# Layer B of a two-layer encoder trunk: the value projection as seven half-size products, and keys split once and doubled by transfers inside SBUF

## The chip, the cores and the metric

The kernel runs on one core of one Trainium2 chip. The metric is device time in microseconds (us) of one execution; lower is better. The engines are named as the profile names them: PE (TensorE, matrix products), DVE (VectorE), ACT (ScalarE), POOL (GpSimd) and SP (SyncE, which issues transfers). Each has an instruction queue of its own and works through it strictly in order.

## The reference, cut to what matters

The input is 512 tokens of width 1024, in float32. Layer A (sparse attention and a squared-ReLU MLP) comes first. Layer B then works on the residual stream `h`:

```
k, v, f_logit = split(rms_norm(h, g_kv) @ w_kv)      # 512x1024 @ 1024x2064
cum = cumsum(log_sigmoid(f_logit + b_f))             # one value per head and token
q = rms_norm(h, g_attn_b) @ w_q                      # 16 heads of 64
logits = q @ k.T / 8 + cum[t] - cum[s], causal       # per head
h = h + (softmax(logits) @ v) @ w_o
h = h + square(relu(rms_norm(h, g_mlp) @ w_up)) @ w_down
```

and a last RMS norm gives the output. The value projection is `v = x @ w_v` with x of 512x1024 and w_v of 1024x1024.

## The kernel before, in words

**Three passes for one product.** Matrix operands are float32r. To keep float32 accuracy each operand is split into a high part (rounded to float32r) and a low part (the rest), and `mm3` issues three matmuls: high by high, high by low, low by high. A split costs one pass of ACT (the high part) and one of DVE (the low part). For weights there is a second way, switched by `lows(stage)`: ACT writes the high part and its negative, and a POOL transfer that adds on arrival (`wlo<-raw`) makes the low part in SBUF.

**What sets the order.** `body` only records operations. `Recorder.schedule` (a list scheduler with cost estimates per operation, priorities from PE's order, and pools of SBUF slots and PSUM banks) then writes the final order of every engine's queue, and `emit` issues them. All instructions therefore carry one source line, L416, in the profile, and are told apart by the names of their tiles.

**Layer B, in the order of PE's work.**

- `afterA` (line 1055) ends layer A's MLP: it normalises h, transposes it through PSUM (`yT`), and splits it twice, into `xq` (scaled with g_attn_b) and `xk` (scaled with g_kv). Both show as `xT` in the profile.
- The query projection (`qp`, `qo`), then the 16 forget-gate logits (`fb`).
- The value projection (line 1108 on): `tokprod` twice, for columns 0 to 511 and 512 to 1023. Each half takes 8 chunks of k, 4 tiles of 128 tokens, 3 passes: 96 matmuls of 128x512. Results (`tp`) are split into `vb`; head pair 4 also gets an unsplit copy `vbf`.
- On DVE, in the meantime, the forget-gate chain: `z`, `e`, `s`, `w2` and their polynomial, then the running sum `cum`. `cum` goes to DRAM (`cd`), comes back as a row per head broadcast over partitions (`ck`), and is transposed on PE (`cb`, `cq`).
- `bias(head)`: POOL makes the decay and mask `bt` from `ck` and `cq`, four `TENSOR_SCALAR` and four `AFFINE_SELECT` a head.
- `kproj(p)`, for 8 pairs of heads: 24 matmuls into `kp`. The logits of a head contract over 128 partitions that hold the 64 rows of k twice (once for the high, once for the low part of q). So each head's 64 rows of `kp` are written to both halves of a tile `kdup`, split into high and low: per pair four ACT casts and four DVE subtractions of 64x512.
- `attn(p)`: logits (`lg`, 8 matmuls a head, 128 to 512 columns wide), sum and minimum on DVE (`l<-lg,bt`), exponent on ACT, reciprocal (`rc`) on DVE, scaling on POOL (`l<-l,rc`), transposes on PE (`pT`), a split (`ph`, `pl`) by ACT and DVE, and the product with v (`pv`, 8 matmuls a head).
- The output projection: 192 matmuls `tp<-whi,qo` and `tp<-wlo,qo`, which also fill PE's gaps in the later pairs. Then layer B's MLP, whose down projection already runs as seven products.

Of the kernel before, what the change touches and what calls it, by code (L numbers as in the profile page):

```python
# [15 lines left out]
T = 512  # L16
# [109 lines left out]
class Recorder:  # L126
# [294 lines left out]
CFG = {  # L421
# [8 lines left out]
def body(ctx, tc, a, out):  # L430
# [19 lines left out]
    p_ps = pool("ps", 8, bass.MemoryType.PSUM, reach=CFG["ps"])  # L450
    p_dr = {n: pool(n, 1, bass.MemoryType.DRAM) for n in ("hd", "cd")}
# [45 lines left out]
    def lows(stage):  # L497
        lo_eng[0] = G if stage in CFG["dl"] else V
# [180 lines left out]
    def unpair(dst, b, scale):  # L679

        up, dn = slice(0, 64), slice(64, 128)
        S.activation(dst[up, 0], b[up], AF.Copy, scale=scale)
# [128 lines left out]
    oT = new_xT("oT")  # L811
    topk(1)
    qprod(1, 0)
    for t in range(NT):
# [3 lines left out]
        for kv in range(4):  # L818
# [38 lines left out]
            else:  # L857

                pv, u, o = bank([128, 4, 128], "pv"), scr([64, 4, 128], "u"), scr([128, 2, 128], "o")
# [6 lines left out]
            split(oT[0][kv][:, :, c], oT[1][kv][:, :, c], o)  # L866
# [16 lines left out]
    mT = None  # L883

    def proj_o(oT, w, g, first):
        tokprod(xl(oT), w, 0, 8, 0, 512, addto(0), order=first)
# [5 lines left out]
        tokprod(xl(oT), w, 0, 8, 512, 512, last, order="t")  # L892
        return xT

    lows("oa")
    xT = proj_o(oT, a["w_o_a"][0], g, "t")


    def mlp(xT, wu, wd, after, last=False):
        lows("up1" if last else "up0")  # L900
        H = T // 2
        tl = [slice(0, H), slice(H, T)]

        share = [htile([128, 512], "share") for _ in range(2)]

        def add(o, b, x):
            V.tensor_tensor(o, b, x, op=OP.add)

        def xop(src):
            out = []  # L910
            for k in range(0, 4, 2):
                hl = tuple(rec.tile(p_x8, [128, 2, H], F32R, n) for n in ("xhi", "xlo"))
                split(hl[0], hl[1], src[:, k:k + 2, :])
                out.append(hl)
            return out

        def wop(src):
            out = []
            for y in src:
                hl = rec.tile(p_wh, [128, 2, 512], F32R, "dhi"), rec.tile(p_wl, [128, 2, 512], F32R, "dlo")  # L920
                split(hl[0], hl[1], y)
                out.append(hl)
            return out

        def sub(o, p, q):
            for x, y, z in zip(o, p, q):
                V.tensor_tensor(x, y, z, op=OP.subtract)

        def part(b, x, w, start, i, c=slice(0, 512), js=range(2)):

            for j in js:
                for k in (2 * j, 2 * j + 1):
                    mm3(b[:, c], tuple(u[:, k % 2, 128 * i:128 * i + 128] for u in x[j]),
                        tuple(u[:, k % 2, c] for u in w[j]), start and k == 0, k == 3, skip_group_check=True)

        def prod(bs, x, w, start, whole=False):
            if whole:
                for i in range(2):
                    part(bs[i], x, w, start, i)
            else:  # L940
                for j in range(2):
                    for i in range(2):
                        part(bs[i], x, w, start, i, js=(j,))

        def banks():
            return [bank([128, 512], "tp") for _ in range(2)]

        for ci in range(4):
# [26 lines left out]
            def raw(j, n):  # L975
                ys = []
                for k in range(f0 + 512 * j, f0 + 512 * j + 512, 256):
                    ys.append(rec.tile(p_wr, [128, 2, 512], F32, "raw"))
# [353 lines left out]
```

## Time and profile before

| | |
|---|---|
| time, median of 3 runs | 1167.9 us (1167.73 to 1167.95) |
| the profiled execution's own time | 1168.06 us |
| its span, first to last instruction | 1166.2 us |
| PE, DVE, ACT, POOL busy, share of the span | 98%, 66%, 64%, 20% |
| value projection on PE | 623.6 to 668 us |
| layer B's attention on PE, first logits to last `pv` | 678.5 to 790.5 us |
| last matmul of the output projection | 825.7 us |

A row of the profile's timeline gives start, duration, engine, line, operation, output<-inputs, the tile's shape and how many stand together; in brackets, how long the engine had been idle and who released it. Matmuls overlap each other: their listed duration (about 390 ns for 128x512) is longer than the distance from one start to the next, so PE's busy share reads near 100% even where it does less than it could. The distance between starts is the number to price a matmul with.

### The profile page before, as it was taken

Reading aid. Unit: us, or ns where it says so; the run is one execution under the profiler, and the core shown is the slowest. Engines: PE = TensorE matmul, PEld = TensorE weight load, DVE = VectorE, ACT = ScalarE, POOL = GpSimd, SP = SyncE. Lnnn points to the kernel's source line nnn. Section 1 sums busy time; section 2 is a strip of 40 time slices with the busy share of each in tenths; the row PEclk is TensorE's granted clock in tenths of the full one; section 3 lists DMA queues with packets and bytes.
Section 4 is the critical chain, followed back from the end, with each engine's and each line's share of the span. In section 5 each row is a group of like instructions: output and inputs, shape, how many; then the busy total and the mean of one; then the engine's idle time right before and its main releaser. Section 6 shows DMA issues by size and latency. Waiting matters only on the chain. (4 is left out here: it accounts for less than half of the span.)

```text
span 1166.2 us, 16382 instructions
## 1 busy us (share of the span) xinstructions
PE 1141.8 (98%) x5687; PEld 948.6 (81%) x5687; DVE 771.8 (66%) x1489; ACT 741.6 (64%) x1396; POOL 236.5 (20%) x391
## 2 busy tenths in 40 slices
PE   8999999999999999999999999999999999999997
PEld 7777787898888888888887878788988888888885
DVE  7899998455736656468656359773568357465596
ACT  8852899665745556559573259996568356465562
POOL 0311454110200200201010068961101002002001
PEclk9999999999999999999999999999999999999999
DMA  9841363782982964957875313768719819739501
GB/s 341 184 91 55 110 181 70 148 235 59 241 242 64 256 186 123 269 150 176 234 173 124 110 37 115 207 169 179 204 68 240 248 56 248 219 88 255 198 19 73
DMA packets 145315, 187.86 MB, mean 161 GB/s; under 512 B 8104, under 2 KB 92096, under 8 KB 145232
## 3 DMA queue, kind: packets, MB, share of 16 engines
q1 hardware_dynamic: 129680, 130.18, 35.5%
q0 software_dynamic: 15552, 56.63, 25.2%
q8 instruction: 45, 0.74, 0.3%
q14 instruction: 38, 0.31, 0.1%
HBM read 125.94 MB, written 4.23 MB: 112 GB/s over the span
## 5 line engine op out<-in xcount | busy, mean ns | idle before, releaser
L416 PE MATMUL up<-xT,whi 128*128 128x512 f32 (+1 forms) x1152 | 323.7, 366 | 0.0
L416 PEld LDWEIGHTS up<-xT,whi 128*128 128x128 f32 x1152 | 207.9, 189 | 34.9
L416 POOL DMA_DIRECT2D wlo<-raw x108 | 95.1, 881 | 692.6 <-ACT wlo L416 339.2
L416 DVE TENSOR_TENSOR dlo<-raw,dhi 128x1024 fp32r<-128x1024 f32 x112 | 136.5, 1227 | 144.5 <-ACT dhi L416 90.3
L416 PE MATMUL up<-xT,wlo 128*128 128x512 f32 (+1 forms) x576 | 210.0, 366 | 0.0
L416 PE MATMUL tp<-dhi,xhi 128*128 128x512 f32 (+1 forms) x452 | 171.9, 390 | 1.2 <-DVE h L416 0.8
L416 PE MATMUL tp<-dlo,xhi 128*128 128x512 f32 (+1 forms) x452 | 171.4, 387 | 0.0
L416 PE MATMUL tp<-dhi,xlo 128*128 128x512 f32 (+1 forms) x452 | 170.8, 388 | 0.0
L416 ACT CAST whi<-raw 128x1024 fp32r<-128x1024 f32 (+2 forms) x124 | 123.9, 1026 | 72.9 <-DMA raw<-in_w_up_dram 63.1
L416 ACT CAST dhi<-raw 128x1024 fp32r<-128x1024 f32 x112 | 116.4, 1047 | 67.1 <-PE up L416 64.1
L416 PE MATMUL tp<-whi,xT 128*128 128x512 f32 (+2 forms) x432 | 125.2, 371 | 2.7 <-DVE r L416 1.6
L416 ACT ACTIVATE wlo<-whi 128x1024 fp32r<-128x1024 f32 x108 | 112.4, 1059 | 20.8 <-DMA wlo<-raw 10.3
L416 PEld LDWEIGHTS up<-xT,wlo 128*128 128x128 f32 x576 | 108.3, 189 | 17.5
L416 DVE TENSOR_TENSOR h<-tp,h 128x512 f32<-128x512 f32 (+1 forms) x97 | 64.7, 680 | 79.0 <-PE tp L416 78.9
L416 PEld LDWEIGHTS tp<-dhi,xhi 128*128 128x128 f32 x452 | 84.8, 188 | 21.7 <-DVE h L416 1.4
L416 PEld LDWEIGHTS tp<-dhi,xlo 128*128 128x128 f32 x452 | 84.7, 188 | 17.3
L416 PEld LDWEIGHTS tp<-dlo,xhi 128*128 128x128 f32 x452 | 84.9, 188 | 16.8
L416 PEld LDWEIGHTS tp<-whi,xT 128*128 128x128 f32 x432 | 77.0, 188 | 14.7 <-ACT whi L416 3.4
L416 DVE TENSOR_TENSOR raw<-raw 128x1024 f32<-128x1024 f32 x64 | 76.6, 1220 | 18.3 <-DMA raw<-in_w_down_dram 17.6
L416 ACT ACTIVATE r<-up 128x512 f32<-128x512 f32 x64 | 37.9, 592 | 79.6 <-PE up L416 79.6
L416 POOL TENSOR_SCALAR l<-l,rc 128x128 f32<-128x128 f32 (+3 forms) x128 | 69.9, 574 | 52.7 <-DVE rc L416 38.3
L416 PE MATMUL tp<-wlo,xT 128*128 128x512 f32 (+2 forms) x216 | 78.4, 372 | 0.5 <-DVE ra L416 0.5
(191 smaller groups left out, 1928.7 us busy)
## 6 DMA issues: line engine op xcount, KB each, us to landing
wlo<-raw POOLq DMA_DIRECT2D x108, 512.0 KB, 8.8
raw<-in_w_down_dram SPq DMA_DIRECT2D x96, 512.0 KB, 10.9
raw<-in_w_up_dram SPq DMA_DIRECT2D x64, 512.0 KB, 7.1
raw<-in_w_kv_b_dram SPq DMA_DIRECT2D x16, 512.0 KB, 6.8
raw<-in_w_in_a_dram SPq DMA_DIRECT2D x12, 512.0 KB, 8.6
raw<-in_w_o_a_dram SPq DMA_DIRECT2D x8, 512.0 KB, 4.4
raw<-in_w_q_b_dram SPq DMA_DIRECT2D x8, 512.0 KB, 7.6
ck<-cd SPq DMA_DIRECT2D x16, 256.0 KB, 3.7
```

What stands on the lines that cost most here:

```text
L416: getattr(self.engs[o.eng], o.fn)(*a, **k)
```

## The change

Two things are changed in layer B; layer A's code is only regrouped into shared helpers (`xop`, `wop`, `part`, `prod` leave `mlp`), and the two output projections keep their old form (`p7` holds only "v").

First, keys. `kproj` splits the 128 rows of a pair once into `kn`, high and low (one ACT cast and one DVE subtraction of 128x512), and four transfers from SBUF to SBUF on SP's queue write each head's 64 rows to both halves of `kdup`.

Second, the value projection. x is cut into blocks X[i,j] (token half i, k half j) and w_v into Y[j,n]; `proj7` forms seven products of 256x512 by 512x512 (24 matmuls each) from sums and differences of blocks, and adds the results. It needs the normalised input unsplit as well: `afterA` writes it to `xv` by 16 more ACT passes from PSUM. Products 1, 2 and 4 use blocks of the existing split `xk`. Weight blocks are combined in place (`raw<-raw`) and split into `dhi`, `dlo`; for products 3, 7 and 4 the low part comes by POOL's transfer. Blocks overwritten by a combination are loaded again (14 loads of 512 KB, before 8).

```diff
 CFG = {
+    "pw": 700, "p7": ("v",), "swap": False, "dup": True,
+    "far": ("v3", "v7", "v4"),
...
+    def wop(src, far=False):
+        out = []
+        for y in src:
+            hl = rec.tile(p_wh, [128, 2, 512], F32R, "dhi"), rec.tile(p_wl, [128, 2, 512], F32R, "dlo")
+            if far:
+                S.copy(hl[0], y)
+                S.activation(hl[1], f32(hl[0]), AF.Copy, scale=-1.0)
+                G.dma_start(hl[1], y, accum_op=OP.add)
+            else:
+                split(hl[0], hl[1], y)
+            out.append(hl)
+        return out
...
+    def proj7(X, ops, w, c0, stage, first, parts, done):
+        far = lambda n: (stage + n) in CFG["far"]
+
+        def op(i, j):
+            return ops[i, j] if ops else xop(X[i, j])
+
+        def raw(j, n):
+            return wraw(w, 0, j, c0 + 512 * n)
+
+        y11 = raw(0, 0)
+        b = banks(p_pw)
+        prod(b, op(0, 0), wop(y11, far("1")), True)
+        for i in range(2):
+            first(i, b[i])
+        prod(b, op(0, 1), wop(raw(1, 0), far("2")), False, True)
+        for i in range(2):
+            done(i, 0, b[i])
+        s1, s2 = ([rec.tile(p_s4, [128, 2, H], F32, n) for _ in range(2)] for n in ("s1", "s2"))
+        each(OP.add, s1, X[1, 0], X[1, 1])
+        sub(s2, s1, X[0, 0])
+        sub(X[1, 0], X[0, 0], X[1, 0])
+        sub(X[0, 1], X[0, 1], s2)
+        sub(y11, raw(0, 1), y11)
+        y22 = raw(1, 1)
+        sub(y22, y22, y11)
+        e = banks(p_pw)
+        prod(e, xop(s2), wop(y22, far("6")), True)
+        for i in range(2):
+            parts(2 + i, 0, e[i])
+        prod(e, xop(s1), wop(y11, far("5")), False)
+        for i in range(2):
+            parts(2 + i, 1, e[i])
+        z22 = raw(1, 1)
+        prod(e, xop(X[0, 1]), wop(z22, far("3")), False, True)
+        for i in range(2):
+            done(i, 1, e[i])
+        y12 = raw(0, 1)
+        sub(y12, z22, y12)
+        b = banks(p_pw)
+        prod(b, xop(X[1, 0]), wop(y12, far("7")), True)
+        for i in range(2):
+            done(2 + i, 1, b[i])
+
+        y21 = raw(1, 0)
+        sub(y21, y21, y22)
+        prod(b, op(1, 1), wop(y21, far("4")), False, True)
+        for i in range(2):
+            done(2 + i, 0, b[i])
...
+    xv = [big([128, 2, T], "xv", F32) for _ in range(4)] if "v" in CFG["p7"] else None
...
+                for i in range(2 if xv else 0):
+                    S.activation(xv[k // 2][:, i, c], b[:, i, :], AF.Copy, scale=gkv[:, k + i:k + i + 1])
...
+    def vfirst(i, b):
+        m1[i] = htile([128, 512], "m1")
+        S.copy(m1[i], b)
+
+    def vpart(t, n, b):
+        pt[t, n] = htile([128, 512], "vp")
+        add(pt[t, n], b, m1[t - 2])
...
+        if CFG["dup"]:
+
+            kn = htile([128, 2, T], "kn", F32R)
+            split(kn[:, 0, :], kn[:, 1, :], b)
+            for e in range(2):
+                for o in range(2):
+                    SP.dma_start(f32(ks[e])[64 * o:64 * o + 64], f32(kn)[64 * e:64 * e + 64])
+            return ks
```

The scheduler rewrites the order of all engines between 560 us and 826 us of the old profile; on PE the instructions of the first 2650 or so and of the last 1711 stand as before. Three places matter below.

PE, where the value projection has ended and the attention begins (`kp` is the key projection, `cb` the transposes of `cum`, `lg` the logits). Before, with 192 value matmuls and 7 of `kp` ahead of it:

```order
L416 MATMUL kp<-xT,whi 128x512
L416 MATMUL cb<-ident,cum 128x16
L416 MATMUL kp<-xT,whi 128x512
L416 MATMUL cb<-ident,cum 128x16 x2
L416 MATMUL kp<-xT,wlo 128x512
L416 MATMUL cb<-ident,cum 128x16
L416 MATMUL kp<-xT,whi 128x512 x2
```

In the changed kernel, with 168 value matmuls and 49 of `kp` ahead:

```order
L416 MATMUL kp<-xT,whi 128x512
L416 MATMUL cb<-ident,cum 128x16 x4
L416 MATMUL lg<-kdup,qo 128x128 x2
L416 MATMUL lg<-kdup,qo 128x256 x2
L416 MATMUL lg<-kdup,qo 128x384 x2
L416 MATMUL kp<-xT,whi 128x512
L416 MATMUL kp<-xT,wlo 128x512
```

`cb` has moved from the 200th to the 218th place after the forget-gate logits, and the first logits follow it at once instead of 36 matmuls later. At the first `pT` 70 matmuls of `kp` were done before, 112 now.

DVE, at the end of the forget-gate chain. Before, the chain stood nearly alone, with two value splits in its last steps:

```order
L416 TENSOR_TENSOR e<-e,s 16x512
L416 TENSOR_TENSOR vb<-tp,vb 128x8x64
L416 TENSOR_TENSOR z<-z,e 16x512
L416 TENSOR_TENSOR vb<-tp,vb 128x8x64
L416 SCALAR_TENSOR_TENSOR cum<-z,zrow 16x512
L416 TENSOR_TENSOR vb<-tp,vb 128x8x64 x2
```

In the changed kernel it stands behind and between the additions of the seven products (`vp`), all value splits and the first key split:

```order
L416 TENSOR_TENSOR vp<-tp,vp 128x512
L416 TENSOR_TENSOR e<-e,w_6665 16x512
L416 TENSOR_TENSOR vb<-vp,vb 128x8x64
L416 TENSOR_SCALAR e<-e 16x512
L416 TENSOR_TENSOR vb<-vp,vb 128x8x64
...
L416 TENSOR_TENSOR kn<-kp,kn 128x512
...
L416 SCALAR_TENSOR_TENSOR cum<-z,zrow 16x512
L416 TENSOR_TENSOR wlo<-raw,whi 128x1024
L416 TENSOR_TENSOR kn<-kp,kn 128x512
```

Between the first `vp` and `cum` stand 4 `wlo`, 10 additions, 6 `vb` and one `kn` beside the chain itself.

SP, the transfers around `cum`. Before:

```order
L416 DMA raw<-in_w_kv_b_dram 128x8x128 x3
L416 DMA cd<-cum 16x512
L416 DMA ck<-cd 128x512 x2
L416 DMA raw<-in_w_kv_b_dram 128x8x128
L416 DMA ck<-cd 128x512 x2
```

In the changed kernel:

```order
L416 DMA raw<-in_w_kv_b_dram 128x8x128 x5
L416 DMA kdup<-kn 64x1024 x4
L416 DMA raw<-in_w_kv_b_dram 128x8x128
L416 DMA cd<-cum 16x512
L416 DMA kdup<-kn 64x1024 x4
L416 DMA ck<-cd 128x512 x5
```

The first `ck` now stands behind the four transfers of the second pair's keys, which wait for `kn`, which DVE writes two instructions after `cum`.

## Rows read from the trace of the kernel before

**Rows 1.** The page's first part: each engine's busy time, share of the span and instructions.

```profile
PE 1141.8 (98%) x5687; PEld 948.6 (81%) x5687; DVE 771.8 (66%) x1489; ACT 741.6 (64%) x1396; POOL 236.5 (20%) x391
```

**Rows 2.** Busy time by stretch: bounds and length in us, then busy us and instructions of PE, PE's weight loads, DVE, ACT, POOL, the granted clock (1.00 is full), the DMA engines' share and GB/s. The stretches are the second half of the query projection, the value projection, the start of the attention, the attention, and the rest of the output projection.

```profile
585.00:624.00 39.00, 38.90 (x221) 32.84 (x220) 18.58 (x36) 29.99 (x48) 6.38 (x8) 1.00 0.76 166
624.00:668.00 44.00, 44.00 (x195) 36.42 (x195) 26.34 (x37) 9.30 (x16) 0.00 (x0) 1.00 0.43 112
668.00:690.00 22.00, 19.96 (x95) 16.05 (x94) 12.42 (x27) 9.93 (x21) 14.37 (x35) 1.00 0.19 49
690.00:790.00 100.00, 97.90 (x557) 80.65 (x557) 81.17 (x217) 94.87 (x229) 76.81 (x165) 1.00 0.52 148
790.00:826.00 36.00, 35.94 (x170) 29.60 (x169) 14.72 (x37) 23.45 (x46) 6.60 (x8) 1.00 0.72 152
```

**Rows 3.** The chain of work that ended last: start, us, what.

```profile
716.45 1.27 PE pv L416 x8
...
750.98 4.72 PE pv L416 x16
...
790.78 21.34 PE tp L416 x94
```

**Rows 4.** PE's timeline: the first value matmul, the first logits, the first transpose of the attention, a block of eight transposes and the instruction after it, the last `pv` pair, and the first matmul of layer B's MLP.

```profile
623.59 0.40 PE L416 MATMUL tp<-whi,xT 128*128 128x512 f32 x1
...
678.50 0.33 PE L416 MATMUL lg<-kdup,qo 128*128 128x128 f32 x2
...
689.20 0.65 PE L416 MATMUL pT<-ident,l 128*128 128x128 f32 x4 [2.04 <-POOL l L416]
...
773.45 1.08 PE L416 MATMUL pT<-ident,l 128*128 128x128 f32 x8
774.28 0.68 PE L416 MATMUL lg<-kdup,qo 128*128 128x256 f32 x3
...
790.33 0.33 PE L416 MATMUL pv<-ph,vb 128*128 128x256 f32 x1
...
825.88 0.40 PE L416 MATMUL up<-xT,whi 128*128 128x256 f32 x2
```

**Rows 5.** Groups of instructions from 664 to 792 us: engine, operation, tiles, shapes and count, then busy us and mean ns of one, then idle us before them and who ended it.

```profile
L416 POOL TENSOR_SCALAR l<-l,rc 128x512 f32<-128x512 f32 (+3 forms) x64 | 36.1, 593 | 18.4 <-DVE rc L416 17.3 <-PE pT L416 1.0
L416 POOL TENSOR_SCALAR bt<-ck,cq 128x512 f32<-128x512 f32 (+3 forms) x64 | 34.6, 568 | 53.8 <-ACT cq L416 48.8 <-DVE mn L416 3.1 <-DVE pl L416 1.0
...
L416 DVE TENSOR_TENSOR kdup<-kp,kdup 64x512 fp32r<-64x512 f32 x32 | 22.0, 688 | 12.6 <-ACT kdup L416 12.1
...
L416 POOL TENSOR_SCALAR_AFFINE_SELECT bt<-bt 128x128 f32<-128x128 f32 x64 | 18.9, 340 | 0.1
L416 ACT CAST kdup<-kp 64x512 fp32r<-64x512 f32 x32 | 18.6, 581 | 11.6 <-PE kp L416 9.2 <-DVE kdup L416 2.1
```

**Rows 6.** DVE's timeline: the start of the forget-gate chain, a weight split and what follows it, the running sum, two value splits.

```profile
624.40 0.74 DVE L416 SCALAR_TENSOR_TENSOR z<-fb,bfc,f 16x512 f32<-16x512 f32 x1 [1.05 <-ACT f L416]
...
635.63 1.21 DVE L416 TENSOR_TENSOR wlo<-raw,whi 128x1024 fp32r<-128x1024 f32 x1
636.77 0.41 DVE L416 TENSOR_SCALAR e<-e 16x512 f32<-16x512 f32 x1
...
645.29 1.20 DVE L416 TENSOR_TENSOR_SCAN cum<-z,zrow 16x512 f32<-16x512 f32 x1
646.42 1.25 DVE L416 TENSOR_TENSOR vb<-tp,vb 128x512 fp32r<-128x512 f32 x2
```

**Rows 7.** Instructions by tile over the whole run (count: least/median/most ns, first and last start): the MLP's split of combined weights on DVE and ACT, its split of combined inputs, and ACT's scaling of the transposed input out of PSUM.

```profile
L416 DVE TENSOR_TENSOR dlo<-raw,dhi x112: 1210/1225/1721, 247.8 to 1136.2; 128x1024 fp32r<-128x1024 f32 x112
...
L416 ACT CAST dhi<-raw x112: 1032/1047/1058, 246.7 to 1121.2; 128x1024 fp32r<-128x1024 f32 x112
...
L416 DVE TENSOR_TENSOR xlo<-s,xhi x32: 678/683/687, 291.7 to 1132.5; 128x512 fp32r<-128x512 f32 x32
...
L416 ACT ACTIVATE xT<-yT,gkv x16: 475/514/541, 567.8 to 591.1; 128x256 fp32r<-128x256 f32 x16
```

**Rows 8.** Transfers: the page's issues (count, KB each, median us from issue to landing), then for `ck` alone the issue's own ns and the least, median and longest landing.

```profile
wlo<-raw POOLq DMA_DIRECT2D x108, 512.0 KB, 8.8
raw<-in_w_down_dram SPq DMA_DIRECT2D x96, 512.0 KB, 10.9
...
raw<-in_w_kv_b_dram SPq DMA_DIRECT2D x16, 512.0 KB, 6.8
...
L416 SPq DMA_DIRECT2D ck<-cd x16: 319/361/1917, 648.1 to 749.4; - x16
...
DMA to landing us min/median/max: 3.2/3.7/8.0
```

**Rows 9.** POOL's timeline: its first work of the attention, and its last scaling.

```profile
670.70 4.15 POOL L416 TENSOR_SCALAR bt<-ck,cq 128x512 f32<-128x512 f32 x8 [48.75 <-ACT cq L416]
674.81 2.01 POOL L416 TENSOR_SCALAR_AFFINE_SELECT bt<-bt 128x128 f32<-128x128 f32 x8
676.81 2.63 POOL L416 TENSOR_SCALAR bt<-ck,cq 128x512 f32<-128x512 f32 x5
...
782.48 2.06 POOL L416 TENSOR_SCALAR l<-l,rc 128x512 f32<-128x512 f32 x4 [1.97 <-DVE rc L416]
```

**Rows 10.** SP's waits from 600 to 800 us: waiting queue, who was waited for, us in total, times, longest.

```profile
SPq L416 <- DVE cum L416: 25.5, 1, 25.5
```

More of the change, by code (lines that the diff above doesn't have):

```diff
@@ L808, in topk @@
         V.tensor_scalar(m, m, -3.2e38, NEG, op0=OP.is_gt, op1=OP.mult)
-    oT = new_xT("oT")
+    oT = [big([128, 2, T], "oT", F32) for _ in range(4)] if "oa" in CFG["p7"] else new_xT("oT")
     topk(1)
@@ new lines, in wop, with each @@
+    def wop(src, far=False):
+        out = []
+        for y in src:
[6 more added lines that the diff above has]
+                split(hl[0], hl[1], y)
+            out.append(hl)
+        return out
+    def each(op, o, p, q):
+        for x, y, z in zip(o, p, q):
+            V.tensor_tensor(x, y, z, op=op)
@@ new lines, in sub, with part, prod @@
+    def sub(o, p, q):
+        each(OP.subtract, o, p, q)
+    def part(b, x, w, start, i, c=slice(0, 512), js=range(2)):
+        for j in js:
+            for k in (2 * j, 2 * j + 1):
+                mm3(b[:, c], tuple(u[:, k % 2, 128 * i:128 * i + 128] for u in x[j]),
+                    tuple(u[:, k % 2, c] for u in w[j]), start and k == 0, k == 3, skip_group_check=True)
+    def prod(bs, x, w, start, whole=False):
+        if whole:
+            for i in range(2):
+                part(bs[i], x, w, start, i)
+        else:
+            for j in range(2):
+                for i in range(2):
+                    part(bs[i], x, w, start, i, js=(j,))
@@ new lines, in proj_o, with addh, first, done @@
+    def proj_o(X, w, g, stage):
+        xT = new_xT()
+        m1 = [htile([128, 512], "m1") for _ in range(2)]
+        def addh(t, n, b):
+            o = h[t][:, 512 * n:512 * n + 512]
+            add(o, b, o)
+        def first(i, b):
+            S.copy(m1[i], b)
+            for t, n in ((i, 1), (2 + i, 0), (2 + i, 1)):
+                addh(t, n, m1[i])
+        def done(t, n, b):
+            addh(t, n, b)
+            if (t, n) in ((0, 1), (1, 1), (2, 0), (3, 0)):
+                norm_T(h[t], rstd(h[t]), g, xT, t)
+        proj7(X, None, w, 0, stage, first, addh, done)
+        return xT
@@ L887, in proj_o, with proj_d @@
+    quad = lambda x: {(i, j): [x[2 * j + k][:, :, tl[i]] for k in range(2)] for i in range(2) for j in range(2)}
+    def proj_d(lhs, w, g, order):
+        tokprod(lhs, w, 0, 8, 0, 512, addto(0), order=order)
         xT = new_xT()
@@ L891, in last @@
             norm_T(h[t], rstd(h[t]), g, xT, t)
-        tokprod(xl(oT), w, 0, 8, 512, 512, last, order="t")
+        tokprod(lhs, w, 0, 8, 512, 512, last, order="t")
         return xT
-    lows("oa")
-    xT = proj_o(oT, a["w_o_a"][0], g, "t")
+    if "oa" in CFG["p7"]:
+        xT = proj_o(quad(oT), a["w_o_a"][0], g, "oa")
+    else:
+        lows("oa")
+        xT = proj_d(xl(oT), a["w_o_a"][0], g, "t")
     def mlp(xT, wu, wd, after, last=False):
         lows("up1" if last else "up0")
-        H = T // 2
-        tl = [slice(0, H), slice(H, T)]
         share = [htile([128, 512], "share") for _ in range(2)]
[L906 to L946, printed above, removed]
         for ci in range(4):
@@ L1244, in attn @@
                 V.tensor_tensor(o[64 * e:64 * e + 64], pv[0:64], u, op=OP.add)
-        split(qo[p][:, 0, :], qo[p][:, 1, :], o)
+        if not oB:
+            split(qo[p][:, 0, :], qo[p][:, 1, :], o)
+        elif p in CFG["pvb"]:
+            S.copy(oB[p // 2][:, p % 2, :], o)
+    oB = [big([128, 2, T], "oB", F32) for _ in range(4)] if "ob" in CFG["p7"] else None
     kss = {0: kproj(0)}
```

112 lines of the change are left out of this document (77 added, 35 removed).

## The prediction, made before the changed kernel ran

> **What bounds the kernel now.** I read first the page's part on engines and then the windows by stretch. PE is busy for 98% of the span [rows 1], and the granted clock is 1.00 (the 2.4 GHz level) in all five stretches [rows 2], so the change has no clock term. Then PE's own timeline, for where that busy time holds work and where it holds waiting. All that changes on PE lies between the first value matmul at 623.59 us and the first `up` at 825.88 us: 202.3 us [rows 4].
>
> Prices: a 512-column matmul costs 21.34/94 = 0.227 us, a head's 8 `pv` 1.27 (0.159 each; a head's 8 `lg` have the same columns), pair 4's 16 `pv` 4.72 [rows 3], a `pT` (774.28 - 773.45)/8 = 0.104 [rows 4]. I price `cb` and `yT` like `pT`. Work: (192 value + 192 `kp` + 192 output projection) x 0.227 = 130.75; 16 heads of `lg` 20.3; 14 of `pv` 17.8; 4.7; 160 `pT` 16.6; 16 `yT` 1.7; 4 `cb` 0.4. Sum 192.25. So 10 us of the 202.3 are lost, and where they are lost decides how much of a saving arrives. Up to the first `pT` at 689.20, 262 matmuls (192 value, 70 `kp`) 59.5, 18 `lg` 2.85 and `cb` 0.4 give 62.75 of 65.6: 2.85 lost, 2.04 of it the wait for POOL's first `l` [rows 4]. After it, 129.5 of 136.7: 7.2 lost. Behind the last `pv` at 790.33 stand 146 matmuls and the `yT`, 34.85 of 35.55, so 6.5 of the 7.2 belong to the attention. There ACT is busy for 94.9, DVE for 81.2 and POOL for 76.8 of 100 us [rows 2].
>
> **The change part by part.** *Value products.* 24 matmuls less: 24 x 0.227 = 5.45 us off PE.
>
> *What feeds them.* Between 585 and 668 us DVE is busy for 18.58 + 26.34 = 44.9 of 83 us, ACT for 39.3 [rows 2]. DVE gains 8 weight combinations and 8 `dlo`. The trace has no two-input DVE instruction on raw weights alone; `dlo`, 1.23 us in the median [rows 7] and 1.14 by distance between starts (636.77 - 635.63, a `wlo` of the same size, [rows 6]), bounds it from above, and half of that is the least I can argue from the `vb` splits of half the size, 1.25/2 = 0.63 [rows 6]. I take 1.14 since the size is the same: 16 x 1.14 = 18.2. Input combinations and their low parts are 16 of 128x512: x 0.63 = 10.1 (by the row's own 0.683 [rows 7], 10.9). Ten additions read from PSUM: x 0.63 = 6.3. Together 34.6, so 79.5 of the 77.6 us that remain: DVE is full, and what doesn't fit lands on the forget-gate chain, next term. ACT gains 16 `xv` x 0.51, 8 `xhi` x 0.6 (a cast of this size is between the 0.51 and the 0.581 of [rows 7, 5]), four weight passes x 1.05 [rows 7] and two `m1`: 18.4 on 39.3, which fits. One hazard on PE: product 2 waits for ACT's copy `m1`, which in ACT's queue stands behind a `dhi` whose block is re-loaded late; a re-load lands 6.8 us after issue [rows 8]. I take 0.5 us for it, bounds 0 and 2.
>
> *The forget-gate chain.* `cum` on DVE ends at 646.4 today, 22.1 us after `z` [rows 6], with PE far from needing it. Chain without two `wlo` (2.3) and the two `vb` (1.25): 18.5. In the changed order there stand behind the first `vp` 4 `wlo` 4.6, 10 additions 6.3, 6 `vb` 3.8 and a `kn` 0.7. The first `vp` needs the 72nd value matmul: 623.6 + 72 x 0.227 = 639.9; 639.9 + 33.9 = 673.8 if the whole chain were behind it, and a microsecond more for waits between small instructions. PE comes to `cb`, the 218th, at 623.6 + 217 x 0.227 = 672.9. So the added wait is 2 us (0 if part of the chain slips ahead of the first `vp`; 4 if `vp` banks come late). Behind `cb` PE has all logits queued, so nothing fills it.
>
> *`ck` and POOL's start.* SP's wait for `cum` is 25.5 us long [rows 10] and moves with it: `cd` issues at about 675. The first `ck` then stands behind four `kdup` transfers, which wait for `kn`, 1.14 (`wlo`) + 0.7 later, and cost four issues of 0.36 [rows 8]: `ck` at 678.3, landed at 682.0 (3.7), at worst 686.3 (8.0). POOL needs 4.15 + 2.01 + four of the next five `bt` at 0.53 (2.63/5), 2.1 [rows 9], and a scaling 0.6: the first `l` is done near 691, at worst 695. PE is at its first `pT` after (168 + 112) x 0.227 + 22 `lg` 3.5 + 0.4 = 67.5 of work, at 691.1, plus 2 + 0.5 of waits and the 0.8 that is lost there today without a named wait: 694.4. So POOL doesn't bind at the median, and the 2.04 wait goes in exchange for the one at `cb`.
>
> The transfers' order weighs against this change by a rule too. SP's queue sat 25.5 us at one transfer for `cum` [rows 10]. The Trainium skill ("DMA: Bandwidth & Descriptors", section "Anatomy of one DMA — SWDGE (gpsimd) path") says that the DMA engines do not wait on semaphores and any wait happens on the issuing sequencer before dispatch; the trace agrees. By that rule the `ck` row pays for `kn` though it doesn't need it; without the rule it would land some 3.3 us sooner, still ahead of PE's need.
>
> *Keys.* A pair's four DVE subtractions of 0.688 become one, and four ACT casts of 0.581 one [rows 5]; by size I take the same for 128 rows. Six pairs fall after 690: DVE -12.4, ACT -10.3 us. The 32 transfers of 256 KB go between SBUF tiles, which the trace doesn't show: nearest rows are `ck` (3.7) below and `w_down` (10.9) above [rows 8]; a gain is excluded, since today no transfer stands there. I take 4, as the size is `ck`'s. What hides them: PE's order has 16 to 31 us of other work between a pair's last `kp` and its first logits (6 for pair 0, where the wait for `cum` lies anyway). Splits 1.3, issues 1.4 and 4 make 6.7, or 13.6 with 10.9: covered. Only pair 6 has less, as its transfers stand on SP behind three loads whose slots PE frees some 8 us ahead.
>
> *Sum.* After the first `pT` PE has 192.25 - 5.45 - 67.5 = 119.3 of work. The lost 7.2 I put at 6.2: ACT is relieved, but POOL starts later (below) and takes most of that back. Bounds 2 and 12. 694.4 + 119.3 + 6.2 = 819.9 against 825.9: **6.0 us less**. The profiled execution took 1168.06, so 1162.1; measured against the median of 1167.9, **1161.9**. Outside this window PE's order is the same.
>
> **The rivals.** *The lost time goes too (0.16).* If ACT at 95% is what makes the attention lose 6.5 us, the relief leaves about 2: 4 more saved, 1158. For it: ACT is the busiest of the three. Against it: POOL is what ended the named wait, and its load is denser now.
>
> *POOL sets the attention, slower (0.08).* POOL's 89.6 us of attention work [rows 5] are the same, but 14.4 lay ahead of 690 [rows 2] and now only its first 8.9. Today it does the other 75.2 in the 94.5 us up to 784.5: 0.80 of the time. It would have 36.1 + 28.1 (52 of 64 `bt`) + 16.5 (56 of 64 selects) = 80.7 from 691 on. At a share of 0.80 it needs 101 us and its last `l` ends at 792; the last `pv` follows 6 us later (790.5 - 784.5), then 130 matmuls and `yT`, 31.2 + 0.7: `up` at 830, 4 slower, **1172**. It decides below a share of 0.83. My forecast needs 0.89. For it: all heads pass POOL in order, with work that cannot start before `ck`. Against it: 17.3 of its 18.4 idle us ahead of the scalings ended with DVE's `rc` [rows 5], so it is paced from outside and can be denser. *In between (0.14)*, a share of 0.86 ends its last `l` at 785 and leaves a gain of 3, 1165; at 0.84 to 0.85, or with `cum` 2 later still, the gain is within 2.3 us (0.12).
>
> *Transfers late (0.05).* If `kdup` takes its upper bound while weights load (DMA share 0.52 [rows 2]) and pairs 5 to 7 come 4 us late each, PE loses 12 us: 1174. It decides from a mean lateness of 2 us at these three. Against it: the margins above.
>
> *The change does nothing for time (in the 0.12).* That the saved matmuls are just waited out at `cb` takes a `cum` at 678, four more than worked out.
>
> **How the numbers follow.** The forecast holds 0.45, with its own range of 1159.5 to 1164. 0.2%, 2.3 us, is what a measurement of this kernel can tell from no change. Faster: 0.45 + 0.16 + 0.14 = 0.75; same 0.12; slower 0.08 + 0.05 = 0.13. Range 1155.5 (lost time at its lower bound of 2, 1157.7, and no wait at `cb`) to 1168.5; what lies above is the two slower cases.
>
> **What would show it.** Right: 168 value matmuls with starts 0.227 apart from 623.6 on; `cb` released by DVE's `cum` at about 675; first `bt` near 682, first `pT` near 694, last `pv` near 788, first `up` near 820; `kdup` landing in about 4 us. Wrong: PE waiting for a `kdup` transfer; a wait in the value stage for `dlo` or `m1` above 2 us; PE idle `<-POOL l` growing over the heads; or the second MLP taking another time than before.

## The result, and the profile after

The changed kernel takes 1177.4 us (median of 4 runs, 1174.5 to 1178.6), the kernel before 1167.9: a ratio of 1.0076, 95% interval 1.0056 to 1.0095. It is slower by 9.4 us; the forecast was 1161.9, in a range that ended at 1168.5.

The page's first part stands against [rows 1], the windows against [rows 2] (the same stretches and columns):

```profile
PE 1142.3 (97%) x5663; PEld 947.0 (80%) x5663; DVE 789.8 (67%) x1507; ACT 744.4 (63%) x1402; POOL 232.3 (20%) x389
```

```profile
585.00:624.00 39.00, 38.08 (x223) 32.97 (x223) 35.15 (x60) 29.01 (x55) 1.98 (x2) 1.00 0.73 208
624.00:668.00 44.00, 43.19 (x188) 34.37 (x187) 37.66 (x48) 25.98 (x35) 5.25 (x6) 1.00 0.55 117
668.00:690.00 22.00, 21.55 (x101) 17.73 (x100) 12.28 (x19) 4.51 (x8) 2.01 (x4) 1.00 0.68 174
690.00:790.00 100.00, 88.87 (x479) 72.00 (x478) 62.99 (x195) 77.34 (x197) 82.31 (x186) 0.95 0.84 216
...
```

The 100 us from 690 on show it at a glance. DVE fell from 81.2 to 63.0 and ACT from 94.9 to 77.3, but PE fell with them, from 97.9 to 88.9; the clock is 0.95 instead of 1.00; and the DMA engines' share rose from 0.52 to 0.84. Part of the fall is that the attention begins 12 us later in this window. From its first `pT` to its last `pv`, before and after, DVE's busy time fell from 81.2 to 67.3 and ACT's from 95.7 to 86.2, about what the key part promised:

```profile
689.20:790.80 101.60, 99.50 (x567) 82.25 (x568) 81.17 (x217) 95.67 (x230) 78.34 (x166) 1.00 0.52 146
```

```profile
700.90:804.70 103.80, 96.44 (x538) 78.99 (x537) 67.28 (x194) 86.20 (x206) 82.14 (x180) 0.96 0.81 205
```

PE's timeline of the changed kernel, at the places of [rows 4], with its longest waits in brackets:

```profile
625.50 0.40 PE L416 MATMUL tp<-dhi,xT 128*128 128x512 f32 x1
...
677.03 0.42 PE L416 MATMUL cb<-ident,cum 16*128 16x16 f32 x4 [0.45 <-DVE cum L416]
...
692.75 1.00 PE L416 MATMUL lg<-kdup,qo 128*128 128x256 f32 x4 [2.02 <-DVE mn L416]
...
697.81 0.58 PE L416 MATMUL lg<-kdup,qo 128*128 128x256 f32 x2 [1.75 <-DVE mn L416]
...
700.96 0.86 PE L416 MATMUL pT<-ident,l 128*128 128x128 f32 x4
...
764.61 0.44 PE L416 MATMUL lg<-kdup,qo 128*128 128x128 f32 x1 [5.04 <-DMA kdup<-kn]
...
767.64 0.63 PE L416 MATMUL tp<-wlo,qo 128*128 128x512 f32 x1
768.07 1.05 PE L416 MATMUL tp<-whi,qo 128*128 128x512 f32 x2
...
804.35 0.28 PE L416 MATMUL pv<-pl,vb 128*128 128x256 f32 x1
...
836.12 0.40 PE L416 MATMUL up<-xT,whi 128*128 128x256 f32 x2
```

| us | before | forecast | after |
|---|---|---|---|
| first value matmul | 623.6 | 623.6 | 625.5 |
| `cb` | 668.8 | 675.4 | 677.0 |
| first `bt` on POOL | 670.7 | 682 | 688.0 |
| first `pT` | 689.2 | 694.4 | 701.0 |
| last `pv` | 790.5 | 788 | 804.4 |
| first `up` | 825.9 | 819.9 | 836.1 |

Behind the first `up` both take the same (1166.2 - 825.9 = 340.3, 1176.6 - 836.1 = 340.5), so all of the loss lies in this table. Against the forecast it is +1.6 us up to `cb`, +4.9 from there to the first `pT`, +9.8 to the last `pv`, and nothing behind it.

SP's timeline around `cum` and around pair 6's keys, the first `bt` on POOL, and what the profile says of the transfers (the issue's own ns, least, median and longest; then the landing in us):

```profile
672.83 3.10 SPq L416 DMA_DIRECT2D kdup<-kn  x4
676.03 1.08 SPq L416 DMA_DIRECT2D raw<-in_w_kv_b_dram  x1
677.16 1.35 SPq L416 DMA_DIRECT2D cd<-cum  x1
678.72 3.39 SPq L416 DMA_DIRECT2D kdup<-kn  x4
683.81 3.30 SPq L416 DMA_DIRECT2D ck<-cd  x5
...
749.47 5.38 SPq L416 DMA_DIRECT2D raw<-in_w_up_dram  x3
754.94 6.06 SPq L416 DMA_DIRECT2D kdup<-kn  x4
```

```profile
687.98 4.13 POOL L416 TENSOR_SCALAR bt<-ck,cq 128x512 f32<-128x512 f32 x8 [40.98 <-DMA ck<-cd]
```

```profile
L416 SPq DMA_DIRECT2D kdup<-kn x32: 467/594/2178, 672.8 to 774.0; - x32
...
DMA to landing us min/median/max: 2.9/5.5/9.7
```

Three things are to be seen. First, `cd`, 32 KB, is issued at 677.16 and `ck`, which needs it, at 683.81: 6.6 us, with four `kdup` and a weight load in flight ahead of it and four `kdup` issued behind it. Before, these two issues lay 1.6 us apart:

```profile
646.52 0.33 SPq L416 DMA_DIRECT2D cd<-cum  x1
648.14 0.83 SPq L416 DMA_DIRECT2D ck<-cd  x2
```

Second, the first `pT` is late by way of ACT. The profile's chain that ended last does not go from `ck` over POOL here, but from `cd` over SP's queue to the load of key weights that stands behind the five `ck`:

```profile
677.16 6.60 DMA cd<-cum
...
687.21 7.65 DMA raw<-in_w_kv_b_dram
694.88 1.06 ACT whi L416
```

ACT had been idle for 9.85 us before this cast. Its first exponent (`l<-l,mn`) stands behind it and starts at 695.83, though the `mn` for it was there at 692.7, and POOL, done with its `bt` at 696.3, waits 3.31 us for `rc`.

Third, pair 6's keys are issued behind three loads of w_up; PE gets them at 764.6, 9.7 us after the first of the four issues, and had run out of work 5.04 us before.

### The profile page after: what moved, and what is told of

Its sections match the earlier page's. It is cut to its first block, busy times and chain, and to the rows that moved or that the text cites. A ratio compares the mean times of both kernels' runs of the same rounds, so it can differ in the third digit from the quotient of the medians.

```text
span 1176.6 us, 16463 instructions
## 1 busy us (share of the span) xinstructions
PE 1142.3 (97%) x5663; PEld 947.0 (80%) x5663; DVE 789.8 (67%) x1507; ACT 744.4 (63%) x1402; POOL 232.3 (20%) x389
## 5 line engine op out<-in xcount | busy, mean ns | idle before, releaser
L416 DVE TENSOR_TENSOR dlo<-raw,dhi 128x1024 fp32r<-128x1024 f32 x120 | 146.0, 1226 | 148.1 <-ACT dhi L416 93.9
L416 PE MATMUL tp<-dhi,xhi 128*128 128x512 f32 (+1 forms) x484 | 183.7, 390 | 1.5 <-DVE h L416 0.8
L416 PE MATMUL tp<-dlo,xhi 128*128 128x512 f32 (+1 forms) x484 | 183.3, 387 | 0.0
L416 PE MATMUL tp<-dhi,xlo 128*128 128x512 f32 (+1 forms) x484 | 182.5, 388 | 0.0
L416 ACT CAST dhi<-raw 128x1024 fp32r<-128x1024 f32 x126 | 130.7, 1047 | 78.5 <-PE up L416 64.1
L416 ACT CAST whi<-raw 128x1024 fp32r<-128x1024 f32 (+2 forms) x116 | 115.6, 1025 | 87.3 <-DMA raw<-in_w_up_dram 64.5
L416 ACT ACTIVATE wlo<-whi 128x1024 fp32r<-128x1024 f32 x100 | 104.2, 1059 | 15.9 <-DMA wlo<-raw 7.1
L416 DVE TENSOR_TENSOR raw<-raw 128x1024 f32<-128x1024 f32 x72 | 86.2, 1221 | 15.7 <-DMA raw<-in_w_down_dram 14.8
L416 PE MATMUL tp<-whi,xT 128*128 128x512 f32 (+2 forms) x304 | 85.9, 363 | 2.7 <-DVE r L416 1.6
L416 ACT ACTIVATE l<-l,mn 128x128 f32<-128x128 f32 (+3 forms) x128 | 71.4, 563 | 4.2 <-DVE mn L416 3.6
L416 DVE TENSOR_TENSOR xlo<-sq,xhi 128x512 fp32r<-128x512 f32 x80 | 52.9, 685 | 14.5 <-ACT xhi L416 14.5
```

The costliest lines, as they stand in the source:

```text
L416: getattr(self.engs[o.eng], o.fn)(*a, **k)
```

## The experiments

Two theories stood at first: T, the transfers between SBUF tiles fill the DMA engines and what the attention waits for comes late; R, the seven products fill DVE, so the attention starts late. Each time below is a median of 4 to 12 runs, and "before" is 1167.9 to 1168.5 beside them.

**Each part alone.**

```diff
-    "p7": ("v",), "dup": True,
+    "p7": (), "dup": True,          # e1: keys only
+    "p7": ("v",), "dup": False,     # e2: values only
```

> Keys split once and doubled by transfers, value projection as before (192 matmuls). Theory T (the 32 transfers between SBUF tiles fill the DMA engines, 5 us a pair, and what the attention waits for arrives late): slower than before, 1171 to 1177. Rival R (the seven products fill DVE, so the running sum, ck and the whole attention start late; the transfers only show it): no slower than before, 1165 to 1168, since DVE and ACT have 10 to 12 us less to do in the attention.

> Value projection as seven products, keys as before (no transfers inside SBUF). Theory T: 5.45 us less on PE, 1.9 us given back by the 16 more ACT passes at the end of layer A, some of the rest at the later start: 1163 to 1167. Rival R: the attention starts about 10 us late here too, so 1172 or more.

Keys alone: 1176.1 (ratio 1.0059, 1.0045 to 1.0072). Values alone: 1173.5 (1.0041, 1.0029 to 1.0054). So both lose, and neither theory foresaw that. With keys alone the first `pT` comes at 686.8, earlier than before, and the last `pv` 115 us later instead of 101; PE waits 9.0 us for `kdup` in all, the longest here:

```profile
730.70 0.41 PE L416 MATMUL lg<-kdup,qo 128*128 128x128 f32 x2 [1.94 <-DMA kdup<-kn]
...
749.66 1.04 PE L416 MATMUL lg<-kdup,qo 128*128 128x128 f32 x6 [1.90 <-DMA kdup<-kn]
...
786.02 0.92 PE L416 MATMUL lg<-kdup,qo 128*128 128x128 f32 x4 [3.14 <-DMA kdup<-kn]
```

With values alone the attention starts late, as R says:

```profile
681.93 0.39 PE L416 MATMUL cb<-ident,cum 16*128 16x16 f32 x4 [1.41 <-DVE cum L416]
...
699.34 0.90 PE L416 MATMUL pT<-ident,l 128*128 128x128 f32 x5 [0.43 <-POOL l L416]
```

Here too the first exponent stands behind a cast of key weights, for which ACT waits 4.40 us, to 693.51. The attention ends at 800.8, 101 us after the first `pT`, the length of before, although PE's order leaves 21 matmuls (4.8 us) less between its first `pT` and last `pv`. The 5.45 us saved are gone into waiting.

**SP's order in the changed kernel.** Three edits of one queue; every other queue keeps its order.

```diff
 kdup x4 (pair 5)
 ck x2
+kdup x4 (pair 6)                    # e3
 raw<-in_w_up x3
-kdup x4 (pair 6)
```

```diff
 cd
+ck x2                               # e4
 kdup x4 (pair 1)
-ck x5
+ck x3
```

```diff
-raw<-in_w_up x3 (between the keys of pairs 5 and 6)
-g, raw<-in_w_up (between the keys of pair 6 and ck)
 kdup x4 (pair 7)
 ck
+raw<-in_w_up x3, g, raw<-in_w_up    # e9; e13 does the same to keys alone
```

> The changed kernel with one edit of SP's order: the four transfers of pair 6's keys stand ahead of three loads of w_up instead of behind them; all other queues are word for word the same. Theory T: the wait of 5.04 us at pair 6's first logits goes, and with it 2.4 us of half clock behind it: 1169 to 1172. Rival R, or POOL as the bound at a share of 0.9: what is saved at pair 6 is waited for elsewhere, 1175 to 1178.

> The changed kernel with one edit of SP's order: the first two ck stand ahead of the four transfers of pair 1's keys instead of behind them. If the queue order delayed POOL's start, cd lands in 2 to 4 us instead of 6.6, the first bt starts near 683 to 685 instead of 688.0 and the two waits for mn (3.8 us, and 1.6 us of half clock behind them) shrink: 1173 to 1175. If the transfers of pair 0's keys, which are in flight before, delay cd by themselves, the first bt stays at 686 or later and the time at 1175 to 1178.

> The changed kernel with one edit of SP's order: four loads of w_up and one of g stand behind the last keys and the last ck of the attention, all other queues word for word the same. Theory Q (small transfers that are wanted at once, kdup and ck, wait in SP's queue and in the DMA engines behind weights that are wanted 40 us later): the wait of 5.04 us at pair 6 goes and no ck is late in its place, 1168 to 1172. Rival L (the 32 transfers themselves fill the engines): the waits come back at other heads, 1175 to 1178.

> Keys by 32 transfers, value projection as before, and the four loads of w_up behind the last keys and the last ck. Of keys alone (1176.1) theory Q holds that what it lost is queueing behind those loads: the waits of PE for kdup fall from 9.0 to below 3 us, 1167 to 1170. If the transfers by themselves fill the engines (L): waits above 5 us, 1173 to 1177.

e3 took the wait at pair 6 away and gained nothing: 1178.7. The chain of waits and PE's timeline of that run show why:

```profile
765.65 8.29 DMA ck<-cd
```

```profile
784.35 1.12 PE L416 MATMUL pT<-ident,l 128*128 128x128 f32 x4 [5.03 <-POOL l L416]
```

The next thing behind these loads that the attention wants was a `ck`. It took 8.3 us, POOL made `bt` and `l` late, and PE waited as long as before, 20 us later. e4 was worse, 1181.7, and above both of its ranges. With nothing between the two on the queue, `ck` was still issued 4.9 us after `cd`, so what was in flight already (pair 0's keys and one weight load) accounts for 3.3 of the 5 us that `cd` lost:

```profile
677.42 1.28 SPq L416 DMA_DIRECT2D cd<-cum  x1
682.31 2.23 SPq L416 DMA_DIRECT2D ck<-cd  x2
```

The first `bt` came 2.0 us earlier (685.96), but its second `ck` landed 3 us behind it. The load of key weights came later too: ACT waited 13.19 us for it, to 697.72, and the first `pT` moved to 703.6. e9 put all these loads behind everything that the attention needs: no wait of PE for `kdup` is left, first `pT` to last `pv` takes 99.2 us instead of 103.4, and the time is 1173.2, 4.1 less:

```profile
700.77 0.66 PE L416 MATMUL pT<-ident,l 128*128 128x128 f32 x4
...
799.93 0.28 PE L416 MATMUL pv<-pl,vb 128*128 128x256 f32 x1
```

e13 does the same for keys alone: waits for `kdup` 3.6 us instead of 9.0, 1170.5 instead of 1176.1. Its runs spread from 1167.2 to 1177.4, wider than any other kernel's. Both came out above the ranges written down for theory Q, but nearer to them than to L's. So queueing behind weights that are wanted later is 4 to 6 us of the loss.

**Half the transfers.**

```diff
-            kn = htile([128, 2, T], "kn", F32R)
-            split(kn[:, 0, :], kn[:, 1, :], b)
             for e in range(2):
+                r, o = slice(64 * e, 64 * e + 64), slice(64 - 64 * e, 128 - 64 * e)
+                split(ks[e][r, 0, :], ks[e][r, 1, :], b[r])
+                SP.dma_start(f32(ks[e])[o], f32(ks[e])[r])
-                for o in range(2):
-                    SP.dma_start(f32(ks[e])[64 * o:64 * o + 64], f32(kn)[64 * e:64 * e + 64])
```

> Value projection as before; each head's keys are split straight into the half where PE left them, by two half-height casts and subtractions a pair, and one transfer a head copies them to the other half: 16 transfers instead of 32. Theory D (transfers between SBUF tiles move only some 215 GB/s at a full DMA share, and fill the engines that ck, weights and the next keys need): PE's waits for kdup fall from 9.0 us to below 3, time 1166 to 1171. Rival D' (it is the length of the path from kp over split, issue and landing to the logits, not the load): the waits stay above 6 us, 1173 to 1177.

> Keys alone with 16 transfers instead of 32 (1175.0) and the four w_up loads behind the last keys. Theory Q: PE's waits for kdup, 9.7 us there, fall below 3, and with half the bytes of the 32 transfers the rest of the attention isn't slowed: 1164 to 1168, at or a little below the kernel before. If the transfers' path or load matters beside the queue: 1169 to 1173.

e7: 1175.0, waits for `kdup` 9.7 us, 7.7 of them in one place, behind four w_up loads. Halving the bytes gave 1.1 us, which is within the spread of e1's runs (1172.2 to 1177.6); by what was written down, rival D' had it. e18 put the loads behind: the waits fell to 2.0, as Q said, and yet the time rose to 1179.5, above both ranges. Its chain of waits, ACT's and PE's timelines:

```profile
771.62 20.18 DMA raw<-in_w_up_dram
```

```profile
791.87 1.04 ACT L416 CAST whi<-raw 128x1024 fp32r<-128x1024 f32 x1 [4.23 <-DMA raw<-in_w_up_dram]
```

```profile
821.92 1.09 PE L416 MATMUL yT<-ident,y 128*128 128x128 f32 x4 [5.15 <-DVE y L416]
```

The w_up loads, now in one heap with POOL's `wlo` transfers and the reload of h, took 20 us to land (the DMA share of that run is 0.95 or more from 770 to 820), ACT stood still for them for 9.4 us, and the end of the attention and the norm behind it waited for ACT. So Q is only half of it. But e13 has such a heap too, with a DMA share of 1.01 or more from 760 to 810, and there ACT waits only 0.3 us for it; why the loads came too late in the one and not in the other is not shown.

**The value stage.** Four kernels ask why `cum` is late. e5 is values alone with the edit shown, and with the chain's priority raised to that of the forget-gate logits (not shown). e10 drops the instructions marked below from the finished order, e17 from e5's code before the order is made; in both, the products are of other numbers.

```diff
+                    if e == "DVE" and x[2] not in chain:     # e5: hold DVE for the chain
+                        soon = [y[0] for y in pend[e] if y[0] < now + 0.15 and y[3] in chain]
+                        if soon:
+                            skipped.append(x)
+                            waits.append(min(soon))
+                            continue
```

```diff
-    "far": ("v3", "v7", "v4"),
+    "far": ("v2", "v6", "v5", "v3", "v7", "v4"),             # e6, beside e5's edit
```

```diff
-        sub(X[1, 0], X[0, 0], X[1, 0])       # e10: the changed kernel in its own order
-        sub(X[0, 1], X[0, 1], s2)            # e17: e5
-        sub(y11, raw(0, 1), y11)
+        raw(0, 1)
-        sub(y22, y22, y11)
...
```

> Value projection as seven products, keys as before; the planner now holds DVE for the forget-gate chain, so that its 24 instructions stand nearly together instead of one by one between splits and additions. Theory S (the products fill DVE, cum comes 35 us later and the attention starts 10 us later, and from first pT to last pv it needs its 101 us whatever PE has to do): cum ends near 650, first pT at 688 to 691, time 1162 to 1165. Rival S' (DVE is simply full: what the chain no longer waits, the low parts of the products and with them PE wait): the first pT moves by 4 us at most, 1169 to 1173.

> As the run with the chain together, and four more low parts of weights (products 2, 5 and 6, of 1.2 us each on DVE) come by POOL's transfer. By S there is nothing left to win on DVE: within 1.5 us of that run. By S' DVE is relieved by 6 instructions, 7 us, of what makes PE wait: 3 to 6 us less than that run.

> The changed kernel with DVE's 8 weight combinations and 4 of its 8 input combinations left out (products 3, 5, 6 and 7 and so the values are other numbers), every queue otherwise in the same order. DVE has 11.6 us less to do. Theory S' (DVE is full in the value stage and its backlog is what makes cum late): cum ends 5 to 10 us earlier, first bt at 680 to 684, first pT at 694 to 698, time 1171 to 1174. Rival (cum is late by its place behind PE's results, not by DVE's backlog): cum within 2 us of 677, time 1176 to 1178.

> As the run with values alone and the chain together (1174.5), with the 8 weight combinations and 4 of the 8 input combinations left out (products 3, 5, 6 and 7 are other numbers); PE's order is the same in both. DVE has 11.6 us less to do ahead of the chain. If it is DVE's backlog that lets PE wait 5.2 us at cb: that wait falls below 1 us and the time to 1168 to 1171. If it is the chain itself, 18 us in one piece just when the products' additions fall due: the wait stays at 4 us or more, 1173 to 1175.

e5: `cum` 15 us earlier than with values alone (666.4), first `pT` 4.4 earlier, and no gain: 1174.5, above both ranges. e10: 11.6 us of DVE's work left out, and `cum` ends 1.0 us earlier (the changed kernel, then e10); 1177.8:

```profile
675.76 1.21 DVE L416 TENSOR_TENSOR_SCAN cum<-z,zrow 16x512 f32<-16x512 f32 x1
```

```profile
674.76 1.21 DVE L416 TENSOR_TENSOR_SCAN cum<-z,zrow 16x512 f32<-16x512 f32 x1
```

e17: the same left out of e5; 1173.7, and PE's wait at `cb` the same to the hundredth (e5, then e17; `m` is the sum that DVE makes right behind `cum`):

```profile
667.05 0.61 PE L430 MATMUL cb<-ident,cum 16*128 16x16 f32 x4 [5.19 <-DVE m L430]
```

```profile
666.20 0.61 PE L430 MATMUL cb<-ident,cum 16*128 16x16 f32 x4 [5.19 <-DVE m L430]
```

DVE's timelines of e5 and of e17 say what held the chain, `z` being its first instruction and `cum` its last:

```profile
646.43 0.74 DVE L430 SCALAR_TENSOR_TENSOR z<-fb,bfc,f 16x512 f32<-16x512 f32 x1 [2.36 <-PE tp L430]
...
665.20 1.21 DVE L430 TENSOR_TENSOR_SCAN cum<-z,zrow 16x512 f32<-16x512 f32 x1
```

```profile
645.59 0.74 DVE L430 SCALAR_TENSOR_TENSOR z<-fb,bfc,f 16x512 f32<-16x512 f32 x1 [2.41 <-PE tp L430]
...
664.35 1.21 DVE L430 TENSOR_TENSOR_SCAN cum<-z,zrow 16x512 f32<-16x512 f32 x1
```

`z` stands behind the first two additions, which wait for PE's second product, and then waits 2.4 us more for a value matmul, although its only operand from PE was ready when the forget-gate logits ended at 625.5, and ACT's copy of that (`f`) at 642.0. Before, it started at 624.4 [rows 6]. So it is not that DVE is full: the chain starts 22 us later by its place in the queue and by a release of PE's, whatever DVE has to do. That this release is the room of `z` in SBUF, taken over from an operand of the products, fits, but no run tried it. e6 cost 16 us: POOL's added transfers made q's low parts late (PE waits 2.2 us for `wlo`), ACT's `dhi` with them (3.1), and the value stage began at 629.8: 1190.1.

**POOL for combinations, and both parts mended.** e8 is the changed kernel with e5's and e7's edits; e11 is e5, and e12 is e8, with this one:

```diff
-        each(OP.add, s1, X[1, 0], X[1, 1])
+        gx(OP.add, s1, X[1, 0], X[1, 1])           # gx: G.tensor_tensor, for all four input combinations
...
-                for i in range(2 if xv else 0):
-                    S.activation(xv[k // 2][:, i, c], b[:, i, :], AF.Copy, scale=gkv[:, k + i:k + i + 1])
+                if xv:
+                    G.tensor_tensor(xv[k // 2][:, :, c], f32(xk[0][k // 2][:, :, c]), f32(xk[1][k // 2][:, :, c]), op=OP.add)
```

> Both parts with both edits: seven products, the chain together, 16 transfers for the keys. If S and D are what made the changed kernel slow, they add up: first pT at 686 to 691, waits for kdup below 3 us, time 1159 to 1166. If one of them only hid another bound (POOL at a share of 0.9, ACT), the attention takes over 104 us from first pT to last pv and the time is 1167 to 1172.

> Value projection as seven products, keys as before, chain held together; the input combinations (8 of 128x512) are made by POOL, which is idle there, and POOL also makes xv as high plus low part instead of ACT's 16 passes from PSUM. By S': PE starts the value stage 1.9 us earlier again, the wait of 5.2 us at cb shrinks by the 5 us that DVE has less to do, time 1165 to 1169. If DVE's share was not the cause, or POOL's instructions slow DVE down: 1172 or more.

> Seven products, chain together, 16 transfers for the keys, and POOL's input combinations and xv. The two edits act on different waits (5.2 us at cb and 1.9 us ahead of the value stage), so 3 to 6 us less than the version without POOL's part: 1165 to 1169, at last not slower than before. If the attention takes back what the start gains: 1170 to 1173.

e8 has both parts with 16 transfers and the chain together: 1171.5 (1.0030, 1.0019 to 1.0040), the best version with the seven products and still slower than before. Its first `pT` to last `pv` takes 102 us with waits of 2.0 for `kdup`; what it has lost lies ahead: 1.8 us at the start and 5.2 at `cb`. e11 and e12 (1183.9 and 1184.2) freed DVE and ACT, and the planner answered by moving `cb` to the 75th place, where PE waits 9.2 us for `cum`. The start stayed at 625.4 although ACT's 16 passes, which e11's expectation blamed for it, were gone.

**The scalings on DVE.**

```diff
-    "bsc": 'G',
+    "bsc": 'V',      # e14: before; e15: the changed kernel with e9's edit; e16: keys alone with it
```

> The kernel before, with the 64 scalings of layer B's attention (and layer A's) on DVE instead of POOL. Question: what sets the 100 us from first pT to last pv. If POOL's chain sets it: that stretch falls below 96 us, time below 1164. If ACT (95% busy) or PE sets it: the stretch stays at 99 to 103 us, time 1166 to 1172.

> The changed kernel with the w_up loads behind and the scalings on DVE, which the keys' split has relieved. If POOL's share was what kept the stretch at 99.4 us in the version with the loads behind (1173.2) although PE has 6 us less to do there: the stretch falls to 92 to 96 us, time 1166 to 1170. If ACT or the length of the softmax chain sets it: 98 to 101 us, 1172 to 1175.

> As the run with keys alone and the loads behind, with the scalings on DVE. If POOL sets the stretch: 3 to 6 us less than that run, and less than before (1162 to 1166). If not: within 2 us of it.

1172.9, 1179.5 and 1184.6: slower in all three. The windows of e14 beside [rows 2]:

```profile
690.00:790.00 100.00, 96.12 (x522) 75.94 (x521) 94.15 (x262) 87.71 (x214) 44.34 (x101) 1.00 0.52 148
```

POOL went from 76.8 to 44.3 and DVE from 81.2 to 94.2, and the first `pT` to the last `pv` took 111 us. So relieving POOL at DVE's cost does not shorten the stretch. Since DVE filled up in exchange, this does not clear POOL in the kernels where it does the scalings; there the trace speaks against it, as POOL itself stood idle for DVE's `rc` for 11.0 us between 690 and 805 in the changed kernel.

## Why the prediction was wrong, point by point

**The products on PE** were right in their work: 168 matmuls, 24 x 0.227 less. The 51.5 us up to `cb`, where 49.3 of work and 2.5 of waits made 51.8, agree in part by luck. The hazard at product 2 was put at 0.5 and took 0.60, but the wait at `cb` was put at 2 and took 0.45; some 1.2 us are lost without a named wait. That the value stage itself would start 1.9 us later wasn't in the sum; PE waits at 568 and 588 us for ACT's `xT`, and why is open.

**"DVE is full, and what doesn't fit lands on the forget-gate chain"** is a wrong mechanism: DVE was busy for 72.8 of the 83 us from 585 to 668, and e10 and e17 took work away and changed nothing. It stays in the account because it would have led to the wrong cure. `cum` came out nearly right (677 against 675) since the sum itself went by the chain's place behind the first `vp`: forecast at 639.9 with 33.9 us to follow, measured at 642.7 with 34.3. One reading of the rows was wrong as well. The trace before does have a two-input DVE instruction on raw weights alone, `raw<-raw` of 128x1024 in layer B's and layer A's MLP, 1.22 us each; by it the weight combinations cost 0.6 us more than forecast, which changes nothing.

**`ck` and POOL's start** is the first step that failed. `ck` was to issue 3.3 us after `cum`; it took 6.8, since `cd` takes 6.6 us instead of 1.6 among the key transfers, and 4.9 in e4, where nothing stands between the two. So `bt` starts at 688.0 and not 682, and that makes the first of PE's two waits for `mn`. The second has a term that the forecast put at nothing: the load of key weights behind the five `ck`, for which ACT stood until 694.88 with the exponents, and DVE's next `mn`, behind it. With these two waits (2.02 and 1.75 us) and some 3 us of half clock, it is the 4.9 us between `cb` and `pT`. The rule of the Trainium skill weighed there ("DMA: Bandwidth & Descriptors", section "Anatomy of one DMA — SWDGE (gpsimd) path": a wait sits on the issuing sequencer) spoke to `kn`, which cost 0.2 us: it was written at 678.69, and the first `kdup` that needs it was issued at 678.72, behind a `cd` whose issue ended at 678.51. What cost was what the DMA engines had ahead of a small transfer.

**Keys: "I take 4, as the size is `ck`'s", "covered"** is the second step that failed. A transfer took 5.5 us in the median, and at the one place that the text itself called short, pair 6, the keys were there 9.7 us after their first issue; with three loads ahead of them in the queue they came 5.04 us late, and 2.2 more went at half clock (the rows at 767.64 and 768.07 are 0.43 apart, not 0.227, from 764.6 to 769.35). The bound of 10.9 stood in the rows, and the value was taken from the other end. So did a transfer between SBUF tiles, which the text says the trace doesn't show: POOL's `wlo<-raw`, 512 KB, 8.8 us to landing [rows 8]. The size was off, but more than the size: every price was for one transfer by itself, and none for what 32 of them take from the others. e3 shows it: the wait is cured and a `ck` is late in its place. (ACT's relief of 10.3 is 10.5 by the text's own prices; nothing hangs on it.)

**"The lost 7.2 I put at 6.2"** is the third step, and the largest term: from the first `pT` to `up` PE lost 15.9 us (135.2 less 119.3 of work). The late keys explain less than half of these 9.7 us more. In e9, where PE waits for no `kdup`, 11.6 are lost (130.9 less 119.3), and with values alone, where there are no such transfers, 12.8 (131.9 less 119.1 by the same prices). What failed is the premise that PE's work sets the time here, so that matmuls saved are time saved.

**The rivals.** "Transfers late" had the mechanism of the key part and 1174, at a chance of 0.05; of the pairs 5 to 7 that it named, only pair 6 was late. "POOL sets the attention" had 1172 by its share; e14 to e16 do not bear it out, nor do they settle it. "The lost time goes too" did not come: with ACT relieved by some 10 us PE was idle longer.

What stays open is the rest of the third step: why the stretch from the first `pT` to the last `pv` takes 99 to 104 us in the kernels with seven products, whatever PE has to do in it (e6 106, e11 105 and e12 109 apart). With values alone ACT is busy for 58.0 of the 60 us from 740 to 800; that ACT sets it is argued, not shown.

## What to carry to other kernels

Price a transfer not only by its own landing but by the engines' time that it takes from all others. Here the DMA share of the stretch before was 0.52, but 0.95 in the 20 us from 750 on, just where pair 6 came late; ask what stands behind the new transfers and how soon that is wanted. In a queue that is worked off in order, a load that is wanted some 20 us later (ACT casts the loads of 749.47 from 769.2 on) belongs behind a small one that is wanted at once. Moving it paid in e9 and e13, and not in e18, where the moved loads came too late themselves. Look also at what stands behind a late small transfer: in the changed kernel that was a weight load, and ACT's exponents waited for it. And matmuls saved ahead of a stretch that PE doesn't set are saved only if that stretch also starts sooner: look first at what starts it.

## What the runs showed of the hardware

The transfers from SBUF to SBUF of 64 partitions each fill the DMA engines at a low rate. In these two microseconds of the changed kernel nothing but pair 0's four `kdup` was under way (DMA share and GB/s are the last two columns):

```profile
674.00:676.00 2.00, 2.00 (x11) 1.65 (x10) 1.90 (x4) 0.00 (x0) 0.00 (x0) 1.00 1.03 215
```

215 GB/s at a full share, where the mixed transfers of 720 to 730 us moved 304 at a share of 1.01. By that rate (an estimate) a pair's 1.05 MB takes all 16 engines for 4.9 us, eight pairs 39 us, where the forecast had counted only four issues and 4 us of latency. The other surprise is the clock. Behind a wait of PE of 5.04 us, and behind two of 2.02 and 1.75 close together, its matmuls ran at half speed, which is the 1.2 GHz level, for some 3 to 5 us (from 764.6 to 769.4 the granted clock was 0.50):

```profile
698.00:700.00 2.00, 2.00 (x7) 1.82 (x7) 1.54 (x7) 1.99 (x7) 0.35 (x1) 0.52 1.11 255
...
760.00:770.00 10.00, 5.39 (x18) 4.54 (x19) 0.18 (x1) 4.05 (x10) 3.83 (x8) 0.66 1.00 241
```

The granted clock was 1.00 in all stretches before, so the forecast had no term for it; pair 6's late transfer cost about one and a half times its lateness (5.04 us of waiting and 2.2 at half clock).
